# Reciprocal roots of the norms on GpSimd with a power instruction, in a two-layer decoder trunk on one core

## The chip, the core and the metric

The kernel runs on one core of a Trainium2 chip. The metric is the device time of one execution in microseconds (us), the median of a few runs. The core has a matrix engine (TensorE, PE in the profile, whose weight loads are PEld), three engines for other arithmetic (VectorE, DVE; ScalarE, ACT; GpSimd, POOL) and SyncE (SP), which issues most of the transfers. Each engine works through its own instructions in a fixed order; an instruction that needs another engine's result waits for a semaphore, and what stands behind it on its engine waits too.

## The reference

Two layers work on 256 tokens of width 1024. Each layer has four norms, before and after the mixer and before and after the MLP, and each is a mean of squares, a reciprocal root and a product:

```python
def _rms_norm(x, g):
    xf = x.astype(jnp.float32)
    y = xf * lax.rsqrt(jnp.mean(xf * xf, axis=-1, keepdims=True) + NORM_EPS)
    return (y * g.astype(jnp.float32)).astype(x.dtype)

def reference(x, w_in, ...):
    for l in range(DEPTH):
        h = _rms_norm(x, g_pre_mix[l])
        parts = jnp.split(h @ w_in[l], split_at, axis=-1)
        ...                                   # sparse attention and forgetting attention
        mix = jnp.concatenate([o_nsa, o_fox], axis=-1) @ w_out[l]
        x = x + _rms_norm(mix, g_post_mix[l])
        h = _rms_norm(x, g_pre_mlp[l])
        y = jnp.square(jax.nn.relu(h @ w_up[l])) @ w_down[l]
        x = x + _rms_norm(y, g_post_mlp[l])
    return x
```

## The kernel before

The 256 tokens are two tiles of 128 rows, t = 0 and 1; a row's square sum is one number per partition, so a reciprocal root is an instruction on a 128x1 operand. Weights come in by DMA as float32 (`wraw`) and are split into a rounded part `whi` (ScalarE) and a rest `wlo` (VectorE, `wlo<-wraw,whi`, two operands in SBUF); each float32 product is then made of fast matmuls on such parts. PSUM banks have four names: `acc`, `x`, `s` and `o`.

No engine's order is written by hand. The kernel's functions record every operation with a `Recorder`; a list scheduler with estimated costs (`_cost`) and due times (`deadlines`) orders all of them, and `RANKS`, a table of (operation number, rank), overrides the rank of single operations at the end. `emit` then writes the operations in that order, so every instruction has the line of `emit` and is told apart by the names of its tiles.

`rsqrt_sum(a, b, eps)` makes 1/sqrt(a + b + eps) from the two halves of a row's square sum. It is called twelve times:

- `first_factors` (layer 0): the squares of the input are summed over the features by a product with a column of one half (`s<-halves,squares`, four small products), copied to `half_sums` by VectorE, and give the factors of both tiles, `r_mix`. `row_scales` turns them into a row on PE (`s<-cst,rsqrt`), and ScalarE and VectorE scale the first chunk's products with them (`kv_tok`, `kS`, `vS`).
- `sandwich` (four times each layer: t = 0 and 1, after the mixer and after the MLP): ScalarE squares the two halves of the product, `acc[0]` and `acc[1]`, with a row sum into `sq` (written `rl,sq`); VectorE makes `mg = acc * gain`; `rsqrt_sum` makes r; VectorE makes `mg = mg * r + xo` in four pieces of 128x256, and PE transposes them (`s<-cst,mg`, four at a time) for the next stage's `xT`. Later X is updated by `x<-m,rsqrt,x`. At the end of the kernel (`store`) there is no next stage: X is updated and stored. There one half of tile 0 is scaled on ScalarE (`m<-m,rsqrt`) and added on GpSimd (`x<-x,m`).
- layer 1's first chunk: `r_mix` from the squares of X (`rms`).

GpSimd otherwise has sixteen AFFINE_SELECT instructions (the causal mask on the `bias` tiles) and 32 DMA issues, 16 a layer, that add a second read of a weight onto `wlo`.

Of the kernel before, what the change touches and what calls it, by code (L numbers as in the profile page):

```python
# [20 lines left out]
AF = mybir.ActivationFunctionType  # L21
OP = mybir.AluOpType
PSUM = bass.MemoryType.PSUM

P = 128
# [30 lines left out]
            "pr", "prT", "x0", "x1", "fV", "hs", "cs", "pcT", "vbig", "vS", "vW", "kstk", "kstv", "rT")  # L56
PAIRS = ("NSSSSSSSSSSSSN", "NSSSSSSSSSSSSSS")
RANKS = (
    (1199, 97914), (1855, 142093), (2445, 288237), (2467, 296098), (2485, 289771), (2685, 346998), (2881, 331053),
    (3625, 402769.65), (3673, 397125), (3771, 402770), (3934, 412549), (4853, 4861), (4862, 4865.000235571775),  # L60
    (4866, 4865), (4868, 574540),
)
EPS = 1e-6

# [133 lines left out]
class Recorder:  # L198
# [21 lines left out]
    def add(self, engine, name, args, kw):  # L220
# [14 lines left out]
        op.tile = _tile(op) if engine == "tensor" else None  # L235
        op.small = engine == "tensor" and not any(v.buf.name.startswith(("whi", "wlo")) for _, v in views)
        op.cost = _cost(op, views) + SLACK.get(engine, 0)
        deps = {} if self.after is None else {self.after: -1e9}
        op.bufs = []
# [245 lines left out]
def _product(name, args, side):  # L485

    n = int(np.prod(args[0].shape[1:]))
    rounded = args[1].dtype == F32R
    if name == "transpose":
        return 85.0 if rounded else 109.0  # L490
    if side > 1:
        return n / 2.4 + 20 if rounded else n / 0.6 + (60 if n >= 256 else 11)
    return max(118.0, n / 2.4 + (14 if n > 256 else 13)) if rounded else max(220.0, n / 0.6 + 7)


def _cost(op, views):

    out = op.args[0] if op.args else op.kw["out"]
    n = int(np.prod(out.shape[1:]))
    part = 100 * (out.shape[0] < P)  # L500
    if op.engine == "gpsimd":
        return 200 + 0.72 * n + 10 * int(np.prod(out.shape[1:-1]))
    if op.engine == "sync":
        v = views[0][1]
        return v.shape[0] * int(np.prod(v.shape[1:])) * 4 / 360.0
    if op.engine == "tensor":
        if op.name == "stretch":
            side = P // min(op.tile)
            return sum(_product(*x[:2], side) for x in op.args[2][::side])
        return _product(op.name, op.args, 1)  # L510
    if op.engine == "vector":
        if op.name == "reciprocal":
            return 60 + 6.5 * n
        if op.name == "tensor_reduce":
            n = int(np.prod(op.args[1].shape[1:]))
        fast = op.name in ("tensor_copy", "tensor_scalar", "memset") and not any(v.buf.psum for _, v in views)
        aps = sum(isinstance(v, View) for v in op.args[2:4]) if op.name == "tensor_scalar" else int(
            op.name == "scalar_tensor_tensor" and isinstance(op.args[2], View))
        return 68 + part + 64 * aps + n * (0.52 if fast else 1.04) + 10 * (op.name == "tensor_tensor_reduce")
    src = op.args[1]  # L520
    aps = sum(isinstance(op.kw.get(k), View) for k in ("bias", "scale", "accum_out"))
    return n / 1.2 + (55 if src.buf.psum else 92) + 93 * aps
# [94 lines left out]
def trunk(nc, A, consts_in, out, sbp, pp, dram):  # L617
    def tile(shape, dtype, name, tag=None, bufs=1):
        return nc.tile(sbp[(tag or name) not in OPERANDS], shape, dtype, name, tag, bufs)
# [4 lines left out]
    def small(shape, name, bufs=2):  # L624
        return tile(shape, F32, name=name, tag=name, bufs=bufs)
# [17 lines left out]
    for l in range(DEPTH):  # L643
# [28 lines left out]
        for u in range(len(PAIRS[l])):  # L672
            b = u % 2 * 2
# [6 lines left out]
        n = len(PAIRS[l])  # L680
# [9 lines left out]
    def weight(*key):  # L690
        return W.get(index[key])
# [13 lines left out]
    for k in range(8):  # L705
# [8 lines left out]
        a = 8 + k * NFIRST - o  # L714
# [18 lines left out]
        nc.tensor.matmul(ps[:, :n], warm[:, :P], warm[:, :n], start=True, stop=True)  # L733
    one_t = small([P, 1], "one", 1)
    nc.vector.memset(one_t, 1.0)
    kst = {}
    kbd = tile([P, 2, 2, 16], F32, name="kbd")
    vrep = tile([P, 2, 4, 2, 16], F32R, name="vrep")
# [29 lines left out]
        nc.scalar.activation(dst[0], src, AF.Copy)  # L768
        nc.vector.tensor_sub(dst[1], src, dst[0].bitcast(F32))

    def rsqrt_sum(a, b, eps=EPS, last=False):

        w = small([P, 5], "rsqrt", 6)
        c, d, y, t, r = (w[:, i:i + 1] for i in range(5))
        nc.vector.tensor_scalar(c, a, eps, None, op0=OP.add)
        nc.vector.tensor_scalar(d, c, -0.5, None, op0=OP.mult)
        nc.scalar.activation(y, b, AF.Ln, bias=c)
        nc.scalar.activation(y, y, AF.Exp, scale=-0.5)
        if last:
            nc.scalar.activation(t, b, AF.Identity, scale=-0.5, bias=d)  # L780
        else:
            nc.vector.tensor_scalar(t, b, -0.5, d, op0=OP.mult, op1=OP.add)
        nc.vector.scalar_tensor_tensor(t, y, t, y, op0=OP.mult, op1=OP.mult)
        nc.vector.scalar_tensor_tensor(r, t, 1.5, y, op0=OP.add, op1=OP.mult)
        return r

    def squares_of_x(t, tag):
# [13 lines left out]
    def to_xT(t, n, xg, xT):  # L801

        ps = psum("s")
        with nc.stretch():
            for k in range(4):
                nc.tensor.transpose(ps[:, k * P:k * P + P], xg[:, k * P:k * P + P], ident)
        split(ps.rearrange("p (k n) -> p k n", k=4), [y[:, 4 * n:4 * n + 4, t * P:t * P + P] for y in xT[:2]])
# [10 lines left out]
    def sandwich(t, acc, g_post, pre=None, xT=None, eps=EPS, store=None):  # L818


        sq = small([P, 2], "sq")
        m, mg = [None, None], [None, None]

        def times(name, n, gain):
            y = tokt(name)
            nc.vector.tensor_mul(y, acc[n], gain[:, half(n)])
            return y

        for n in range(2):
            junk = small([P, 512], "rl")  # L830
            nc.scalar.activation(junk, acc[n], AF.Square, scale=1.0 / 32.0, accum_out=sq[:, n:n + 1])
            if pre:
                mg[n] = times("mg", n, pre[0])
            if n == 0 and not pre:
                m[0] = times("m", 0, g_post)
        r = rsqrt_sum(sq[:, 0:1], sq[:, 1:2], eps, store is not None)
        if not pre:
            m[1] = times("m", 1, g_post)
        if pre:
            xg = []  # L840
            for n in range(2):
                xg.append(mg[n])
                for c in (0, 256):
                    a = n * 512 + c
                    nc.vector.scalar_tensor_tensor(xg[n][:, c:c + 256], mg[n][:, c:c + 256], r,
                                                   pre[1][t][:, a:a + 256], op0=OP.mult, op1=OP.add)
            yield
            for n in range(2):
                to_xT(t, n, xg[n], xT)
            yield  # L850
        for n in range(2):
            if pre:
                m[n] = times("m", n, g_post)
            if store is not None and t == 0 and n == 1:
                nc.scalar.activation(m[n], m[n], AF.Copy, scale=r)
                nc.gpsimd.tensor_add(X[t][:, half(n)], X[t][:, half(n)], m[n])
            else:
                nc.vector.scalar_tensor_tensor(X[t][:, half(n)], m[n], r, X[t][:, half(n)],
                                               op0=OP.mult, op1=OP.add)
            if store is not None:  # L860
                nc.sync.dma_start(store[:, half(n)], X[t][:, half(n)])
        yield
# [35 lines left out]
    def first_factors():  # L898
        ps = psum("s")
        for t in range(NT):  # L900
            nc.tensor.matmul(ps[:, t:t + 1], squares[:, t * P:t * P + P], half_t, start=True, stop=True)
        w = small([P, 2], "half_sums", 1)
        nc.vector.tensor_copy(w, ps[:, :2])
        return [rsqrt_sum(w[:, t:t + 1], w[:, t:t + 1]) for t in range(NT)]
# [5 lines left out]
    for l in range(DEPTH):  # L910
# [517 lines left out]
        if first:  # L1428
            for n, _ in enumerate(in_chunk(0, evac0)):
                if n == 11:  # L1430
                    nc.after = nc.ops[-1]
                    par.update(zip(("smT", "bias", "w2"), load_params(0)))
                    nc.sync.dma_start(cst[:, C_TRI:], consts_in[:, C_TRI:])
                    nc.after = None
                    r_mix = first_factors()
        else:

            for n, _ in enumerate(in_chunk(0, evac0, by_token=True)):
                if n == 6:
                    urgent(carry)  # L1440
                    next(carry)
                    for t in range(NT):
                        r_mix[t] = rsqrt_sum(*squares_of_x(t, "rm"))
# [257 lines left out]
        for u in range(len(PAIRS[l])):  # L1701
            fc, b = (u + 2) // 2, u % 2 * 2
# [7 lines left out]
            a = acts.pop(u)  # L1710
            w = W.pair(index[l, "dn", u // 2, b], PAIRS[l][u] == "S")
# [51 lines left out]
        n = len(PAIRS[l])  # L1763
        for u in range(n, 14):
# [3 lines left out]
            fc, b = u // 2, u % 2 * 2  # L1768
            act = [acts.pop(u)]
            for k in range(2):  # L1770
                w = weight(l, "dn", fc, b + k)
# [78 lines left out]
```

## Time and profile before

| | |
|---|---|
| median of 3 runs | 599.23 us (599.04 to 599.94) |
| span of the profiled execution | 597.2 us |
| PE busy | 589.6 us, 99% |
| DVE busy | 561.8 us, 94% |
| ACT busy | 493.0 us, 83% |
| POOL busy | 38.8 us, 6% |
| chain that ended last | 98% PE |
| mean granted TensorE clock | 0.998 |

The profile is of one execution; the span is from its first to its last instruction, and the 2.0 us to the median of the runs lie outside it (the page gives no other time of that execution). Busy time is a union of the instructions' spans. A matmul's end is modelled: 128x512 matmuls are listed with some 0.39 us but start 0.23 us apart, so PE that is shown as busy may still wait a little between two starts. The chain is followed back from the last instruction to what released each step.

### The profile page before, as it was taken

Reading aid. Unit: us, or ns where it says so; the run is one execution under the profiler, and the core shown is the slowest. Engines: PE = TensorE matmul, PEld = TensorE weight load, DVE = VectorE, ACT = ScalarE, POOL = GpSimd, SP = SyncE. Lnnn points to the kernel's source line nnn. Section 1 sums busy time; section 2 is a strip of 40 time slices with the busy share of each in tenths; the row PEclk is TensorE's granted clock in tenths of the full one; section 3 lists DMA queues with packets and bytes.
Section 4 is the critical chain, followed back from the end, with each engine's and each line's share of the span. In section 5 each row is a group of like instructions: output and inputs, shape, how many; then the busy total and the mean of one; then the engine's idle time right before and its main releaser. Section 6 shows DMA issues by size and latency. Waiting matters only on the chain.

```text
span 597.2 us, 9917 instructions
## 1 busy us (share of the span) xinstructions
PE 589.6 (99%) x3312; PEld 492.7 (82%) x3312; DVE 561.8 (94%) x1212; ACT 493.0 (83%) x899; POOL 38.8 (6%) x53
## 2 busy tenths in 40 slices
PE   9999999999999999999999999999999999999995
PEld 7988887788888888888888888777888888888884
DVE  7899999989999999999799999988999999999997
ACT  7677888677999999998667959884889999999984
POOL 0000200001100001010000021000110010101000
PEclk9999999999999999999999999999999999999999
DMA  8996629729988878989348762584598879887621
GB/s 318 380 356 196 262 83 299 259 70 294 282 238 284 237 252 255 277 246 289 112 138 280 256 207 109 165 295 142 130 299 248 276 231 287 235 271 239 181 36 71
DMA packets 39427, 135.64 MB, mean 227 GB/s; under 512 B 4656, under 2 KB 4816, under 8 KB 39376
## 3 DMA queue, kind: packets, MB, share of 16 engines
q1 hardware_dynamic: 34768, 118.23, 56.4%
q0 software_dynamic: 4608, 16.78, 15.7%
q8 instruction: 26, 0.43, 0.3%
q14 instruction: 25, 0.20, 0.1%
HBM read 133.92 MB, written 1.07 MB: 226 GB/s over the span
## 4 chain that ended last, share of the span: by engine, by line
PE 98%; DMA 1%; DVE 0%; ACT 0%; issue 0%; DVEq 0%
PE s L454 42%; PE acc L454 26%; PE x L454 21%; PE o L454 10%; DMA first<-in_first_dram 1%; DVE x L454 0%; DVE m L454 0%; DVEq L1846 0%; ACT xT L454 0%; DVE rsqrt L454 0%; ACT rl L454 0%
## 5 line engine op out<-in xcount | busy, mean ns | idle before, releaser
L454 ACT ACTIVATE whi<-wraw 128x1024 fp32r<-128x1024 f32 (+2 forms) x188 | 180.5, 978 | 18.4 <-PE acc L454 6.7
L454 DVE TENSOR_TENSOR wlo<-wraw,whi 128x1024 fp32r<-128x1024 f32 (+2 forms) x156 | 171.0, 1105 | 4.0 <-ACT whi L454 3.5
L454 PE MATMUL s<-xT,whi 128*128 128x512 f32 x448 | 111.2, 390 | 0.0
L454 PEld LDWEIGHTS s<-xT,whi 128*128 128x128 f32 x448 | 83.9, 188 | 17.6
L454 DVE TENSOR_TENSOR wlo<-wsum,whi 128x1024 fp32r<-128x1024 f32 x52 | 63.4, 1221 | 2.4 <-ACT whi L454 2.1
L454 PEld LDWEIGHTS s<-xT,wlo 128*128 128x128 f32 x448 | 61.1, 190 | 4.4
L454 PE MATMUL s<-xT,wlo 128*128 128x256 f32 x448 | 62.5, 282 | 0.0
L454 ACT ACTIVATE whi<-wsum 128x1024 fp32r<-128x1024 f32 x52 | 55.0, 1057 | 8.9 <-PE s L454 8.6
L454 POOL DMA_DIRECT2D wlo<-in_w_up_dram x32 | 27.9, 872 | 384.7 <-ACT wlo L454 159.7
L454 PE MATMUL x<-whi,aS 128*128 128x512 f32 x128 | 49.2, 391 | 0.0
L454 ACT ACTIVATE pr<-pr,st 128x256 f32<-128x256 f32 (+1 forms) x96 | 42.8, 449 | 6.8 <-DVE st L454 6.8
L454 PE MATMUL acc<-whi,aS 128*128 128x512 f32 x128 | 45.9, 392 | 0.0
L454 PE MATMUL s<-whi,aS 128*128 128x512 f32 x104 | 37.6, 391 | 0.0
L454 DVE TENSOR_TENSOR wsum<-wraw,wsum 128x512 f32<-128x512 f32 x52 | 35.8, 688 | 0.8
L454 PE MATMUL x<-whi,xT 128*128 128x512 f32 x112 | 35.6, 395 | 0.4 <-ACT xT L454 0.4
L454 PE MATMUL acc<-whi,xT 128*128 128x512 f32 (+1 forms) x128 | 35.6, 350 | 0.0
L454 ACT ACTIVATE y<-s 128x512 f32<-128x512 f32 x56 | 32.7, 584 | 2.8 <-PE s L454 2.4
L454 ACT ACTIVATE wlo<-wraw 128x1024 fp32r<-128x1024 f32 x32 | 33.6, 1051 | 1.4 <-PE o L454 1.1
L454 PE MATMUL acc<-xT,whi 128*128 128x512 f32 x128 | 34.3, 397 | 0.0
L454 DVE TENSOR_TENSOR wsum<-wraw 128x1024 f32<-128x1024 f32 x26 | 31.7, 1220 | 0.0
L454 DVE TENSOR_TENSOR aS<-quads,aS 128x896 fp32r<-128x896 f32 (+3 forms) x31 | 31.4, 1013 | 0.0
L454 ACT ACTIVATE aS<-quads 128x896 fp32r<-128x896 f32 (+3 forms) x31 | 27.5, 887 | 4.2 <-DVE quads L454 3.7
(259 smaller groups left out, 1271.7 us busy)
## 6 DMA issues: line engine op xcount, KB each, us to landing
wraw<-in_w_up_dram SPq DMA_DIRECT2D x64, 512.0 KB, 5.3
wraw<-in_w_down_dram SPq DMA_DIRECT2D x64, 512.0 KB, 5.9
wraw<-in_w_in_dram SPq DMA_DIRECT2D x36, 512.0 KB, 5.2
wlo<-in_w_up_dram POOLq DMA_DIRECT2D x32, 512.0 KB, 7.0
wraw<-in_w_out_dram SPq DMA_DIRECT2D x16, 512.0 KB, 4.1
w<-in_cmp_w_k_dram SPq DMA_DIRECT2D x8, 512.0 KB, 6.0
w<-in_cmp_w_v_dram SPq DMA_DIRECT2D x8, 512.0 KB, 5.8
bias<-sums SPq DMA_DIRECT2D x8, 384.0 KB, 5.3
```

What stands on the lines that cost most here:

```text
L454: getattr(getattr(self.nc, op.engine), name)(*[real(v) for v in args], **{k: real(v) for k, v in kw.items()})
```

## The change

`rsqrt_sum` had two VectorE instructions that prepare (`a + eps` and its product with -0.5), a logarithm and an exponential on ScalarE, and a Newton step of three VectorE instructions (in the last norm one of them on ScalarE). Now it has three GpSimd instructions: `c = a + eps`, `d = b + c`, `r = d ^ -0.5`, the last a TENSOR_TENSOR whose second operand is a 128x1 tile `power` that VectorE fills once. The cost rule of the scheduler gets another estimate for TENSOR_TENSOR on GpSimd. `RANKS` holds other entries, 42 where there were 15, and with this the whole order is another.

```diff
+    (10, 8.9985), (15, 43116.8677), (17, 43116.8654), (20, 1529.1849), (56, 54.0011), (61, 64.0017),
...
     if op.engine == "gpsimd":
+        if op.name == "tensor_tensor" or op.name == "tensor_add":
+            return 200 + 2.1 * n
         return 200 + 0.72 * n + 10 * int(np.prod(out.shape[1:-1]))
...
+    power = small([P, 1], "power", 1)
+    nc.vector.memset(power, -0.5)
...
-    def rsqrt_sum(a, b, eps=EPS, last=False):
-        w = small([P, 5], "rsqrt", 6)
-        c, d, y, t, r = (w[:, i:i + 1] for i in range(5))
-        nc.vector.tensor_scalar(c, a, eps, None, op0=OP.add)
-        nc.vector.tensor_scalar(d, c, -0.5, None, op0=OP.mult)
-        nc.scalar.activation(y, b, AF.Ln, bias=c)
-        nc.scalar.activation(y, y, AF.Exp, scale=-0.5)
-        if last:
-            nc.scalar.activation(t, b, AF.Identity, scale=-0.5, bias=d)
-        else:
-            nc.vector.tensor_scalar(t, b, -0.5, d, op0=OP.mult, op1=OP.add)
-        nc.vector.scalar_tensor_tensor(t, y, t, y, op0=OP.mult, op1=OP.mult)
-        nc.vector.scalar_tensor_tensor(r, t, 1.5, y, op0=OP.add, op1=OP.mult)
+    def rsqrt_sum(a, b, eps=EPS):
+        w = small([P, 3], "rsqrt", 6)
+        c, d, r = (w[:, i:i + 1] for i in range(3))
+        nc.gpsimd.tensor_scalar(c, a, eps, None, op0=OP.add)
+        nc.gpsimd.tensor_scalar(d, b, c, None, op0=OP.add)
+        nc.gpsimd.tensor_tensor(r, d, power, op=OP.pow)
         return r
...
-        r = rsqrt_sum(sq[:, 0:1], sq[:, 1:2], eps, store is not None)
+        r = rsqrt_sum(sq[:, 0:1], sq[:, 1:2], eps)
```

In the rows of the orders below, a name before the arrow is written and the names behind it are read; xN stands for N alike in a row.

The first place is `first_factors`. On VectorE, around the copy of the sums (`half_sums`), before:

```order
L454 COPY half_sums<-s 128x2
L454 TENSOR_TENSOR wlo<-wraw,whi 128x576
L454 TENSOR_SCALAR rsqrt<-half_sums 128x1 x2
L454 TENSOR_SCALAR rsqrt<-rsqrt 128x1 x2
L454 TENSOR_SCALAR rsqrt<-half_sums,rsqrt 128x1 x2
L454 TENSOR_TENSOR wlo<-wraw,whi 128x1024
L454 SCALAR_TENSOR_TENSOR rsqrt<-rsqrt 128x1 x4
L454 TENSOR_SCALAR vS<-x,rsqrt 128x128 x2
```

Now, on the same engine:

```order
L459 TENSOR_TENSOR wlo<-wraw,whi 128x576
L459 COPY half_sums<-s 128x2
L459 TENSOR_TENSOR wlo<-wraw,whi 128x1024
L459 TENSOR_SCALAR vS<-x,rsqrt 128x128 x2
L459 TENSOR_TENSOR rope<-kS,cst 128x32
```

The ten small instructions of the two roots are gone from VectorE, and a 128x1024 split stands right behind the copy. GpSimd has these at its start, ahead of its masks:

```order
L459 TENSOR_SCALAR rsqrt<-half_sums 128x1 x2
L459 TENSOR_SCALAR rsqrt<-half_sums,rsqrt 128x1 x2
L459 TENSOR_TENSOR rsqrt<-rsqrt,power 128x1 x2
L459 AFFINE_SELECT bias<-bias 128x2x128 x8
```

On PE, what now stands between the products that sum the squares (`s<-halves,squares`, right ahead of the first row here) and the turn of the roots into a row (`s<-cst,rsqrt`):

```order
L459 MATMUL acc<-whi,xT 128x288
L459 MATMUL acc<-wlo,xT 128x288
L459 MATMUL acc<-whi,xT 128x288 x2
L459 MATMUL acc<-wlo,xT 128x288
L459 MATMUL acc<-whi,xT 128x288 x2
L459 MATMUL acc<-wlo,xT 128x288
L459 MATMUL acc<-whi,xT 128x288 x2
L459 MATMUL acc<-wlo,xT 128x288
L459 MATMUL acc<-whi,xT 128x288 x2
L459 MATMUL acc<-wlo,xT 128x288
L459 MATMUL acc<-whi,xT 128x288
L459 MATMUL s<-cst,rsqrt 128x128 x2
```

That is 15 matmuls; before, 30 such matmuls stood there.

The second place is `sandwich` after the mixer of layer 0, tile 0 (banks `x`). On VectorE before:

```order
L454 TENSOR_TENSOR mg<-x,gains 128x512
L454 TENSOR_SCALAR rsqrt<-sq 128x1
L454 TENSOR_SCALAR rsqrt<-rsqrt 128x1
L454 TENSOR_TENSOR mg<-x,gains 128x512
L454 TENSOR_SCALAR rsqrt<-sq,rsqrt 128x1
L454 SCALAR_TENSOR_TENSOR rsqrt<-rsqrt 128x1 x2
L454 SCALAR_TENSOR_TENSOR mg<-mg,rsqrt,xo 128x256 x3
```

Now:

```order
L459 TENSOR_TENSOR mg<-x,gains 128x512
L459 TENSOR_TENSOR wsum<-wraw 128x1024
L459 TENSOR_TENSOR mg<-x,gains 128x512
L459 SCALAR_TENSOR_TENSOR mg<-mg,rsqrt,xo 128x256 x4
L459 TENSOR_TENSOR wlo<-wraw,whi 128x1024
```

The small instructions are gone, and a 128x1024 sum of weights stands between the two `mg`. On PE the first transposition `s<-cst,mg` of this place stood behind 16 matmuls into `acc` that follow the last one into `x`; now it stands behind 13.

The third place is the end of the kernel. ScalarE before:

```order
L454 ACTIVATE rl,sq<-x 128x512 x2
L454 ACTIVATE rsqrt<-sq,rsqrt 128x1 x2
L454 ACTIVATE rsqrt<-rsqrt 128x1
L454 ACTIVATE rl,sq<-acc 128x512
L454 ACTIVATE m<-m,rsqrt 128x512
L454 ACTIVATE rl,sq<-acc 128x512
L454 ACTIVATE rsqrt<-sq,rsqrt 128x1 x2
L454 ACTIVATE rsqrt<-rsqrt 128x1
```

ScalarE now, where the product with r comes ahead of both squares of tile 1:

```order
L459 ACTIVATE aT<-h_6911 128x512
L459 ACTIVATE wsum<-x 128x512
L459 ACTIVATE rl,sq<-x 128x512 x2
L459 ACTIVATE m<-m,rsqrt 128x512
L459 ACTIVATE rl,sq<-acc 128x512 x2
```

On GpSimd the addition `x<-x,m` was the last instruction; now it stands between the roots of the two tiles:

```order
L459 TENSOR_SCALAR rsqrt<-sq,epsr 128x1
L459 TENSOR_SCALAR rsqrt<-sq,rsqrt 128x1
L459 TENSOR_TENSOR rsqrt<-rsqrt,power 128x1
L459 TENSOR_TENSOR x_808<-x_808,m 128x512
L459 TENSOR_SCALAR rsqrt<-sq,epsr 128x1
L459 TENSOR_SCALAR rsqrt<-sq,rsqrt 128x1
L459 TENSOR_TENSOR rsqrt<-rsqrt,power 128x1
```

The root of tile 1 thus waits on GpSimd for the addition of tile 0.

More of the change, by code (lines that the diff above doesn't have):

```diff
@@ L58 @@
 RANKS = (
-    (1199, 97914), (1855, 142093), (2445, 288237), (2467, 296098), (2485, 289771), (2685, 346998), (2881, 331053),
-    (3625, 402769.65), (3673, 397125), (3771, 402770), (3934, 412549), (4853, 4861), (4862, 4865.000235571775),
-    (4866, 4865), (4868, 574540),
[8 rows of a table added]
 )
```

7 rows, old and new, of the table RANKS are left out of this document.

## The prediction

> **What bounds the kernel now.** I read the busy shares first, then the chain of waits by engine, then PE's own waits, then the span in three windows (before PE's first real product, to the end of its last, and the rest).
>
> ```profile
> span 597.2 us, 9917 instructions
> PE 589.6 (99%) x3312; PEld 492.7 (82%) x3312; DVE 561.8 (94%) x1212; ACT 493.0 (83%) x899; POOL 38.8 (6%) x53
> PE 98%; DMA 1%; DVE 0%; ACT 0%; issue 0%; DVEq 0%
> PE o L454 <- PEq L1840: 0.8, 1, 0.8
> PE x L454 <- ACT xT L454: 0.4, 1, 0.4
> ...
> 4.87:590.74 585.87, 585.87 (x3302) 489.74 (x3302) 557.75 (x1200) 489.91 (x892) 37.34 (x48) 1.00 0.73 228
> 590.74:597.20 6.46, 0.00 (x1) 0.00 (x0) 3.03 (x7) 1.26 (x5) 1.27 (x1) 0.78 0.44 164
> ```
>
> The chain lies on PE for 98%. PE waited 1.2 us in all (us in total, times, longest), of which 0.8 us before the program's first product; that leaves 0.4 us between 4.87 and 590.74. In the window rows the first number is the length and the second PE's busy time: PE fills 585.87 us of 585.87, at a granted clock of 1.00. The two orders hold the same 3312 matmuls in the same shapes. So the change can't shorten the middle by more than that one wait of 0.4 us and some 0.1 us of changes from one bank to another; everything else that it can do there is to make PE wait for a root. A gain must come from the 6.46 us after PE, where the last root stands.
>
> **What is removed.** Per root two small VectorE instructions and a Newton step go, and a logarithm and an exponential on ScalarE (in the rows on one tile: fewest, median and most ns):
>
> ```profile
> L454 DVE SCALAR_TENSOR_TENSOR rsqrt<-rsqrt x24: 145/185/220, 20.2 to 592.4; 128x1 f32<-128x1 f32 x24
> L454 DVE TENSOR_SCALAR rsqrt<-sq,epsr x4: 204/206/208, 293.7 to 590.5; 128x1 f32<-128x1 f32 x4
> L454 ACT ACTIVATE rsqrt<-rsqrt x12: 186/203/205, 19.0 to 591.9; 128x1 f32<-128x1 f32 x12
> ```
>
> About five VectorE instructions of 0.15 to 0.2 us and two of ScalarE, twelve times: some 10 us of VectorE and 6 us of ScalarE work. Of that nothing counts in itself, since PE hides both engines outside the end of the kernel: I put it at 0.
>
> **What is added: the price on GpSimd.** The trace of before has no 128x1 arithmetic and no power on POOL. The nearest rows:
>
> ```profile
> L1840 POOL MEMSET const-float32-0.0<- 128x1 f32 x1 | 0.1, 99 | 0.2 <-issue 0.2
> L454 POOL TENSOR_SCALAR_AFFINE_SELECT bias<-bias x16: 404/432/1537, 58.9 to 361.6; 128x256 f32<-128x256 f32 x16
> L454 POOL TENSOR_TENSOR x<-x,m 128x512 f32<-128x512 f32 x1 | 1.3, 1269 | 19.4 <-ACT m L454 19.4
> 58.68 1.21 DVE L454 TENSOR_TENSOR wlo<-wraw,whi 128x1024 fp32r<-128x1024 f32 x1
> 58.91 1.25 POOL L454 TENSOR_SCALAR_AFFINE_SELECT bias<-bias 128x256 f32<-128x256 f32 x1 [58.46 <-DVE st L454]
> 65.56 0.42 DVE L454 TENSOR_TENSOR fkT<-acc,fkT 128x256 f32<-128x256 f32 x1
> 65.56 0.41 POOL L454 TENSOR_SCALAR_AFFINE_SELECT bias<-bias 128x256 f32<-128x256 f32 x1 [5.05 <-PE acc L454]
> 354.82 1.54 POOL L454 TENSOR_SCALAR_AFFINE_SELECT bias<-bias 128x256 f32<-128x256 f32 x1 [3.67 <-ACT cs L454]
> 354.86 1.22 DVE L454 TENSOR_TENSOR wlo<-wraw,whi 128x1024 fp32r<-128x1024 f32 x1
> ```
>
> From below: a MEMSET of 128x1 takes 0.10 us. From above: an AFFINE_SELECT of 256 columns takes 0.41. One column with an operand to read lies nearer to the MEMSET; I take 0.2 us for each of the three, the power included, and keep 0.10 and 0.41 for the range. A product on ScalarE that ended at 590.72 let GpSimd start at 590.80 (rows of the end, below), so a hop between engines is 0.08.
>
> The same fence shows a second cost. The AFFINE_SELECT of 0.41 us took 1.25 and 1.54 us where VectorE ran `wlo<-wraw,whi`, with both operands in SBUF, and ended 0.27 us behind it (58.91 + 1.25 = 60.16 against 59.89; 356.36 against 356.08). Beside a VectorE product that reads one operand from PSUM (`fkT<-acc,fkT`) it took 0.41. So GpSimd stood still until VectorE's instruction had ended.
>
> **The first factors (layer 0).** Before:
>
> ```profile
> 17.18 0.50 PE L454 MATMUL s<-halves,squares 128*128 128x1 f32 x4
> 17.72 0.16 DVE L454 COPY half_sums<-s 128x2 f32<-128x2 f32 x1
> 17.80 0.76 DVE L454 TENSOR_TENSOR wlo<-wraw,whi 128x576 fp32r<-128x576 f32 x1
> ...
> 21.61 0.38 PE L454 MATMUL s<-cst,rsqrt 128*128 128x128 f32 x2
> ```
>
> PE starts the sums at 17.18 and turns the roots at 21.61, 4.43 us later, with 30 matmuls of 288 columns between: less 0.4 for the four small products, 0.134 each. Now 15 stand between, so the first turn is due 4.43 - 15 x 0.134 = 2.42 us after the sums, the second 0.1 later. What the roots need: the copy starts 0.54 after the sums; the 128x1024 split that now follows on VectorE starts 0.08 behind it, as `wlo` does at 17.80, and takes 1.22, to 1.84. The first c is released at about 0.78, into the split, and is held to its end; half its own 0.2 remains (1.94). Five more instructions make 1.0, and the hop 0.1: 3.04, against 2.52. That makes PE wait 0.5 us. At 0.10 per instruction it is 0, at 0.41 it is 1.7 (1.84 + 0.28 + 2.05 + 0.1 - 2.52).
>
> The rule for this is in the Trainium skill, page "SBUF — State Buffer", section "Who interferes with whom": a VectorE instruction with two inputs in SBUF contends with a GpSimd instruction that reads SBUF, and whoever issues first holds the shared ports to its end. The trace agrees (1.25 us against 0.41). By the rule the sum has the 0.5 above and the time is 599.5; without it the roots would be there at 0.78 + 1.2 + 0.1 = 2.1, the wait would be 0 and the time 599.0.
>
> **The roots in the middle.** Layer 0 after the mixer, tile 0, is the tightest kind:
>
> ```profile
> 122.00 0.62 PE L454 MATMUL acc<-whi,oT 128*128 128x512 f32 x2
> 122.20 0.60 ACT L454 ACTIVATE rl<-x 128x512 f32<-128x512 f32 x1 [0.22 <-PE x L454]
> 122.70 0.20 ACT L454 ACTIVATION_READ_ACCUMULATOR rl<-x 128x1 f32 x1
> 124.29 1.28 DVE L454 SCALAR_TENSOR_TENSOR mg<-mg,rsqrt,xo 128x256 f32<-128x256 f32 x3
> 125.64 0.60 PE L454 MATMUL s<-cst,mg 128*128 128x128 f32 x4
> ```
>
> From the first matmul behind the bank's end (122.00) to the first transposition were 3.64 us and 16 matmuls; with 13 it is 3.64 - 3 x 0.228 = 2.96 (3.64 over 16 is 0.228 each). Counted from the bank's end, the square sum is out at 0.90. GpSimd's c would start at 0.98, but VectorE's new `wsum<-wraw` of 128x1024 stands between the two `mg`, and it too reads SBUF twice. By the order the first half's bank ends seven matmuls sooner (-1.6); its square sum (0.2 + 0.8) is out at -0.6, `mg` takes 0.69 and the sum, with the 1.21 of `wlo`, runs from 0.1 to 1.3. So c is held to 1.3 and ends at 1.4, r at 1.8, with a hop 1.9. The second `mg` runs from 1.3 to 2.0, so the root is no later than that; two pieces of three in 1.28 are 0.86 and a hop makes 2.94, against 2.96: no wait, and nothing to spare. At 0.41 r comes at 2.5: a wait of 0.5. The two other places of tile 0 have 13 matmuls too and no such sum: 0.98 + 0.6 + 0.08 = 1.66, with 0.94 for pieces and hop 2.6; at 0.41 3.23, a wait of 0.27 each. Tile 1 has 3.0 to 3.5 us, some 0.3 in all at 0.41. So 0 at 0.2 us, and 1.3 at 0.41. PE's matmuls hide these roots; without them the pieces and transpositions would be late by what is missing. On GpSimd itself a root would be late behind its DMA issues, but they lie elsewhere:
>
> ```profile
> 70.17 0.77 POOL L454 TENSOR_SCALAR_AFFINE_SELECT bias<-bias 128x256 f32<-128x256 f32 x2 [1.13 <-DVE gz L454]
> 130.88 1.01 POOL L454 DMA_DIRECT2D wlo<-in_w_up_dram  x1 [59.95 <-DVE mg L454]
> 273.51 0.88 POOL L454 DMA_DIRECT2D wlo<-in_w_up_dram  x1 [6.71 <-ACT wlo L454]
> 349.91 1.24 POOL L454 TENSOR_SCALAR_AFFINE_SELECT bias<-bias 128x256 f32<-128x256 f32 x2 [75.52 <-DVE gh L454]
> ```
>
> Layer 0's last mask is at 70, its first DMA issue comes behind the roots after the mixer (122 to 130), the last ends some 20 us before the roots of the MLP (293.7, among the removed rows above).
>
> **The end of the kernel.**
>
> ```profile
> 588.56 0.20 ACT L454 ACTIVATION_READ_ACCUMULATOR rl<-x 128x1 f32 x1
> 590.01 0.71 ACT L454 ACTIVATE m<-m,rsqrt 128x512 f32<-128x512 f32 x1
> 590.78 0.60 ACT L454 ACTIVATE rl<-acc 128x512 f32<-128x512 f32 x1
> 590.80 1.27 POOL L454 TENSOR_TENSOR x<-x,m 128x512 f32<-128x512 f32 x1 [19.44 <-ACT m L454]
> 591.27 0.19 ACT L454 ACTIVATION_READ_ACCUMULATOR rl<-acc 128x1 f32 x1
> 591.50 0.69 DVE L454 TENSOR_TENSOR m<-acc,gains 128x512 f32<-128x512 f32 x1
> 592.55 1.42 DVE L454 SCALAR_TENSOR_TENSOR x<-m,rsqrt,x 128x512 f32<-128x512 f32 x2
> ```
>
> Before, the last square sum was out at 591.46 and its root let VectorE start at 592.55: 1.09 us. Three instructions and two hops would be 0.76. But two other things come in. ScalarE now does `m<-m,rsqrt` ahead of both squares of tile 1: tile 0's sum is out at 588.76, its root at 588.76 + 0.76 = 589.52, `m` at 590.23, and two squares of 0.68 each (590.78 to 591.46) end at 591.60. And GpSimd adds `x<-x,m` ahead of the three instructions: 590.31 to 591.58, just in time. So the root is there at 591.60 + 0.76 = 592.36, and the last product starts 0.2 us sooner. At 0.10 it is 0.33 sooner, where `m<-acc,gains` (to 592.19) becomes the later of the two. At 0.41 (1.39 with hops) the same working gives root 590.15, `m` 590.86, squares 592.22, root 593.6: 1.1 later.
>
> **The sum.** 0.5 - 0.2 = +0.3 on a span of 597.2. The median of the runs lies 2.03 above that span, and the page gives no other time of this execution, so I carry the difference over: 597.5 + 2.0 = 599.5. All at 0.10, with PE's wait of 0.4 and the bank changes of 0.1 gone too: 0 - 0.33 - 0.5 = -0.8, 598.4. All at 0.41: 1.7 + 1.3 + 1.1 = +4.1, 603.3.
>
> **Rivals.** Slow power (slower): one instruction, `r = d ^ -0.5`, is not like an addition but takes as long on one column as POOL's addition on 512 takes, 1.27 us, 1.07 more than assumed. At the first factors it stands twice in the chain (0.5 + 2.1 = 2.6), at the end its two roots add up (2.0 with the working above), and six sandwiches miss 0.2 to 0.7 each (3.4): +8.0, 607. For it speaks that no row shows a power on POOL; against it that the long row has 512 columns. It decides from 0.42 us for the power alone: at 0.22 too much, four times in the two tight places (0.88), with +0.3, it passes 1.2 us. All three alike pass it from 0.28. A dearer first call belongs here: the first AFFINE_SELECT took 0.84 more than a free one, which VectorE's split explains, since that at 354.82 wasn't the first and took longer; 0.84 more at the first factors would be 600.3. The Trainium skill ("GPSIMD Engine Reference", "Instruction dispatch") gives some 6 us for the first call of freshly loaded code; no row here shows one, and the sum with it would be 605.
>
> No block, or cheap instructions: the copy's release comes first, or 0.10 us is the price. Then PE doesn't wait: 598.4 to 599.0, still no measurable change. For it speak the MEMSETs; against it the two blocked AFFINE_SELECT.
>
> Faster by over 0.2%, which is 1.2 us and about what a measurement of this kernel can tell from no change: it needs the whole 0.33 at the end, the 0.4 of PE's wait, and 0.5 more from waits that the profile doesn't list, some gap in PE's starts: 598.0 or less. Against it stands 585.87 of 585.87.
>
> **How the numbers follow.** My case, a wait of half a microsecond at the first factors nearly paid back at the end: 0.40, 599.5. No block or cheap: 0.22. Instructions of 0.28 to 0.41 us, +1.2 to +4: 0.20. Slow power or a first call of microseconds: 0.10. Faster than 598.0: 0.08. So faster 0.08, within 0.2% 0.62, slower 0.30. The range 598.4 to 603.3 takes the ends of the unknown price and leaves out the slow power and most of the faster case.
>
> **What would show it.** Right: from the start of `s<-halves,squares` to `s<-cst,rsqrt` about 2.9 us, with PE waiting some 0.5 for the root; the first GpSimd instruction on `half_sums` over 0.8 us long and the other five about 0.2; no new PE waits at `s<-cst,mg`; last `x<-m,rsqrt,x` within 0.9 us of the last square sum. Wrong: a power of 0.4 us or more, PE waits at many `s<-cst,mg`, or an addition `x<-x,m` that holds the last root.

## The result, and the profile after

The changed kernel takes 606.46 us (median of four runs, 606.25 to 607.04) against 599.59 us for the kernel before on the same chip: ratio 1.0118, 95% interval 1.0105 to 1.0130, so 6.9 us slower. I had predicted 599.5 us, with a range up to 603.3 and a chance of 0.30 for slower. The profiled execution has a span of 604.8 us against 597.2, 7.6 us more.

The page of the changed kernel begins, and PE's waits are:

```profile
span 604.8 us, 9887 instructions
PE 592.9 (98%) x3312; PEld 494.9 (82%) x3312; DVE 553.8 (92%) x1155; ACT 487.7 (81%) x873; POOL 56.8 (9%) x89
PE 95%; POOL 2%; DVE 1%; ACT 1%; issue 0%; POOLq 0%; DVEq 0%; ACTq 0%
PE s L459 <- POOL rsqrt L459: 3.8, 4, 2.6
PE o L459 <- PEq L1842: 0.8, 1, 0.8
```

VectorE has 8.0 us less to do (561.8 to 553.8) and ScalarE 5.3 less, and nothing came of it. POOL, which had no share in the chain that ends last, now has 2%. PE's list of waits names the cause: four waits for a root that GpSimd makes, 3.8 us in all, one of them 2.6. All four are at `s<-cst,rsqrt`, two at the first factors of layer 0 and two at layer 1's first chunk; no transposition `s<-cst,mg` of the six sandwiches in the middle is among them.

The costs of GpSimd's instructions, on one tile (fewest, median and most ns, first and last start):

```profile
L459 POOL TENSOR_TENSOR rsqrt<-rsqrt,power x12: 550/567/572, 21.9 to 599.6; 128x1 f32<-128x1 f32 x12
L459 POOL TENSOR_SCALAR rsqrt<-sq,rsqrt x8: 282/282/397, 125.8 to 599.2; 128x1 f32<-128x1 f32 x8
L459 POOL TENSOR_SCALAR rsqrt<-sq x4: 221/222/676, 124.1 to 428.9; 128x1 f32<-128x1 f32 x4
```

The first instruction takes 0.22 us, the second 0.28, the power 0.57: 1.07 for the three, where I had 0.6. And one second instruction, at layer 1's first chunk, takes 4.46 us. The timeline there (start, length, instruction):

```profile
309.54 1.41 DVE L459 SCALAR_TENSOR_TENSOR x<-m,rsqrt,x 128x512 f32<-128x512 f32 x2
310.45 4.46 POOL L459 TENSOR_SCALAR rsqrt<-rms,rsqrt 128x1 f32<-128x1 f32 x1 [1.34 <-ACT rl L459]
310.86 3.90 DVE L459 TENSOR_TENSOR wlo<-wraw,whi 128x576 fp32r<-128x576 f32 x5
312.64 0.39 PE L459 MATMUL x<-whi,xT 128*128 128x512 f32 x1
315.61 0.32 PE L459 MATMUL s<-cst,rsqrt 128*128 128x128 f32 x1 [2.59 <-POOL rsqrt L459]
316.95 0.32 PE L459 MATMUL s<-cst,rsqrt 128*128 128x128 f32 x1 [0.22 <-POOL rsqrt L459]
```

GpSimd's instruction starts at 310.45, while VectorE is in the second of seven instructions that follow each other without a break (309.54 to 314.76) and all read two operands from SBUF. It ends at 314.91, behind the last of them. The power follows, and PE turns the root at 315.61, 3 us after the start of its last other matmul (312.64). What came behind that wait stands in the windows (length, PE, PEld, DVE, ACT and POOL busy, granted clock, DMA):

```profile
312.00:315.60 3.60, 1.02 (x5) 0.52 (x3) 2.76 (x4) 0.64 (x4) 3.47 (x2) 1.00 0.82 265
315.60:317.20 1.60, 1.36 (x9) 1.13 (x10) 0.16 (x1) 1.60 (x3) 1.07 (x3) 1.00 0.86 241
317.20:320.60 3.40, 3.40 (x17) 3.39 (x16) 2.78 (x7) 2.88 (x6) 0.00 (x0) 0.51 1.02 377
```

For 3.4 us PE ran at a granted clock of 0.51: about 3.4 x 0.49 = 1.7 us more lost, without any wait.

The first factors and the end of the kernel, which answer to the rows shown of before:

```profile
19.06 0.50 PE L459 MATMUL s<-halves,squares 128*128 128x1 f32 x4
19.60 0.16 DVE L459 COPY half_sums<-s 128x2 f32<-128x2 f32 x1 [1.31 <-PE s L459]
19.68 1.23 DVE L459 TENSOR_TENSOR wlo<-wraw,whi 128x1024 fp32r<-128x1024 f32 x1
19.85 1.14 POOL L459 TENSOR_SCALAR rsqrt<-half_sums 128x1 f32<-128x1 f32 x1 [19.42 <-DVE half_sums L459]
21.38 0.54 POOL L459 TENSOR_SCALAR rsqrt<-half_sums,rsqrt 128x1 f32<-128x1 f32 x2
21.87 1.09 POOL L459 TENSOR_TENSOR rsqrt<-rsqrt,power 128x1 f32<-128x1 f32 x2
22.50 0.32 PE L459 MATMUL s<-cst,rsqrt 128*128 128x128 f32 x1 [0.84 <-POOL rsqrt L459]
23.02 0.32 PE L459 MATMUL s<-cst,rsqrt 128*128 128x128 f32 x1 [0.20 <-POOL rsqrt L459]
...
597.27 0.39 PE L459 MATMUL acc<-whi,aT 128*128 128x512 f32 x1
597.57 1.26 POOL L459 TENSOR_TENSOR x<-x,m 128x512 f32<-128x512 f32 x1 [0.84 <-ACT m L459]
598.44 0.20 ACT L459 ACTIVATION_READ_ACCUMULATOR rl<-acc 128x1 f32 x1
598.81 0.29 POOL L459 TENSOR_SCALAR rsqrt<-sq,epsr 128x1 f32<-128x1 f32 x1
...
600.16 1.42 DVE L459 SCALAR_TENSOR_TENSOR x<-m,rsqrt,x 128x512 f32<-128x512 f32 x2 [0.78 <-POOL rsqrt L459]
```

At the first factors the split that follows the copy holds the first instruction from 19.85 to 20.99 (0.22 without it), and the first turn comes 3.44 us after the sums; 2.42 were free. The second turn is 0.52 behind the first instead of 0.1. That is 1.4 us. At the end the last square sum is out at 598.64 and the product starts at 600.16, 1.52 us later; it was 1.09. From the start of PE's last matmul to the end of the span it is 604.8 - 597.27 = 7.5 us, against 597.2 - 590.36 = 6.8: 0.7 more.

So the 7.6 us are: first factors 1.4; layer 1's first chunk 3.0 of lateness at the two turns and 1.7 of slow clock, 4.7 in all; the end 0.7. The rest, 0.8, is mostly of two parts. PE's first matmuls ran slowly for 0.4 us longer than in the profile of before (the second pair started at 5.85 instead of 5.50); profiles of the kernels below show between 0 and 0.5 of it, so it isn't the change. Some 0.3 lies near 50 us; it is there in every kernel below that has the new order and makes the first factors' roots on GpSimd, and gone where VectorE and ScalarE make them, and I haven't followed it further.

### The profile page after: what moved, and what is told of

Read it like the earlier page. It is cut to its first block, busy times and chain, and to the rows that moved or that the text cites. A ratio compares the mean times of both kernels' runs of the same rounds, so it can differ in the third digit from the quotient of the medians.

```text
span 604.8 us, 9887 instructions
## 1 busy us (share of the span) xinstructions
PE 592.9 (98%) x3312; PEld 494.9 (82%) x3312; DVE 553.8 (92%) x1155; ACT 487.7 (81%) x873; POOL 56.8 (9%) x89
## 3 DMA queue, kind: packets, MB, share of 16 engines
HBM read 133.92 MB, written 1.07 MB: 223 GB/s over the span
## 4 chain that ended last, share of the span: by engine, by line
PE 95%; POOL 2%; DVE 1%; ACT 1%; issue 0%; POOLq 0%; DVEq 0%; ACTq 0%
PE s L459 41%; PE acc L459 24%; PE x L459 19%; PE o L459 11%; POOL rsqrt L459 2%; DVE wlo L459 0%; DVE qS L459 0%; ACT rl L459 0%; POOL x L459 0%; ACT whi L459 0%; DVE fqT L459 0%; DVE x L459 0%; ACT m L459 0%; DVEq L1848 0%; POOLq L1848 0%
```

## The experiments

The theory: GpSimd's instructions read SBUF, and while VectorE works through instructions with two operands in SBUF, one behind the other, they stand still; at the two places where PE has little other work this decides, and a wait of over 2 us also lowers PE's clock. Two rivals: the power's own price makes the loss; the new order of the whole program does, whoever makes the roots.

**The new order with the old roots.** All twelve chains back on VectorE and ScalarE, in the changed kernel's order:

```diff
-        nc.gpsimd.tensor_scalar(c, a, eps, None, op0=OP.add)
-        nc.gpsimd.tensor_scalar(d, b, c, None, op0=OP.add)
-        nc.gpsimd.tensor_tensor(r, d, power, op=OP.pow)
+        # in their places: c, d | Ln, Exp, t | the two steps of Newton
```

> The changed kernel's order, but all twelve roots made as before by VectorE and ScalarE (logarithm, exponential, Newton step), put where the GpSimd instructions stood; the two of the first factors right behind the copy of the sums. Theory (GpSimd's instructions are held by trains of VectorE instructions with two SBUF operands, and are dearer than assumed): the loss goes with GpSimd, so 599 to 600.5 us, PE waits for roots at most 1 us in all, no slow clock at 316 to 321 us. Rival 1 (the new order itself costs, whoever makes the root): 604 to 606. Rival 2 (the power's own 0.57 us is the loss): the same 599 to 600.5, it is told apart by the next kernels.

It took 604.13 us (ratio 1.0074, 1.0059 to 1.0089). My theory's figure is missed, and the time lies in the range of the rival that the new order costs (604 to 606). PE no longer waits at the first factors and there is no slow clock, but the old chains, dropped into places laid out for three instructions, are late elsewhere:

```profile
PE s L494 <- DVE rsqrt L494: 1.3, 1, 1.3
PE s L494 <- DVE mg L494: 0.6, 2, 0.3
```

The 1.3 us are at layer 1's first chunk, where ScalarE's logarithm stood behind a weight split of 1.06 us, and the end was 1.3 us longer than before. The kernel doesn't tell theory and order apart, since it tests my placement as well; the next ones do.

**A multiplication for the power.** The root is left out; every instruction, place and wait stays.

```diff
-        nc.gpsimd.tensor_tensor(r, d, power, op=OP.pow)
+        nc.gpsimd.tensor_tensor(r, d, power, op=OP.mult)
```

> The changed kernel with a multiplication in place of the power (this leaves out the root, so the numbers it makes are another's; every instruction, wait and place is the same). The TENSOR_TENSOR on 128x1 takes about 0.3 us in place of 0.57. Theory (blocked instructions): the waits for blocked instructions stay, so only 0.3 to 0.5 us less at each of the first factors, layer 1's first chunk and the end: 605.2 to 605.9 us, the second instruction of layer 1's first root still over 4 us long. Rival (the power's price makes the loss): 600 to 602.

603.16 us (ratio 1.0054, 1.0033 to 1.0074): 3.3 us less than the changed kernel. Neither figure was met.

```profile
L472 POOL TENSOR_TENSOR rsqrt<-rsqrt,power x12: 191/192/194, 21.5 to 597.1; 128x1 f32<-128x1 f32 x12
309.29 4.44 POOL L472 TENSOR_SCALAR rsqrt<-rms,rsqrt 128x1 f32<-128x1 f32 x1 [1.38 <-ACT rl L472]
PE s L472 <- POOL rsqrt L472: 2.6, 2, 2.2
```

The power costs 0.57 - 0.19 = 0.38 us more than a product on one column. By the times of PE's starts it is in series twice at the first factors (0.75 gained there) and twice at the end (0.7 gained), and shortens the wait and the slow clock at layer 1 (0.8 together). About 0.4 more is the start of PE's clock in that profile. So the power's price is a real part, some 2.3 us. But the blocked instruction is as long as it was, 4.44 us, and PE still waits 2.2 us for it.

**Breaks in VectorE's train.** MEMSETs between the five splits at layer 1's first chunk:

```diff
+        for op, n in zip(wlo[k:], (1, 3, 2, 2)):      # the first four of the five splits
+            for _ in range(n):
+                ops.insert(ops.index(op) + 1, self.made("vector", "memset", self.gap, 0.0))
```

> The changed kernel with eight MEMSETs of 128x192 put on VectorE between the five weight splits at layer 1's first chunk (1, 3, 2 and 2 of them behind the first four). They are extra work, about 1.6 us, but a MEMSET reads no SBUF. Theory (GpSimd gets no turn between two VectorE instructions that follow each other with two SBUF operands): the instruction of 4.46 us ends in the first gap, at about 312 us instead of 314.9, the power in the second, and PE waits for this root under 0.8 us instead of 2.6; with no long wait no slow clock follows: 602 to 603.5 us. Rival (something else delays that instruction, or GpSimd is served between two instructions anyway): nothing won, 606 to 607.

602.93 us (ratio 1.0056, 1.0041 to 1.0071): eight instructions more on VectorE, and 3.5 us faster than the changed kernel.

```profile
309.96 2.05 POOL L477 TENSOR_SCALAR rsqrt<-rms,rsqrt 128x1 f32<-128x1 f32 x1 [1.34 <-ACT rl L477]
310.39 0.74 DVE L477 TENSOR_TENSOR wlo<-wraw,whi 128x576 fp32r<-128x576 f32 x1
311.12 0.22 DVE L477 MEMSET gap<- 128x192 f32 x1
311.26 0.69 DVE L477 TENSOR_TENSOR wlo<-wraw,whi 128x576 fp32r<-128x576 f32 x1
311.94 0.87 DVE L477 MEMSET gap<- 128x192 f32 x3
312.10 0.57 POOL L477 TENSOR_TENSOR rsqrt<-rsqrt,power 128x1 f32<-128x1 f32 x1
312.72 0.32 PE L477 MATMUL s<-cst,rsqrt 128*128 128x128 f32 x1 [0.18 <-POOL rsqrt L477]
```

The instruction ends at 312.01 instead of 314.91, and PE's wait for this root is 0.18 us. The second tile's root still waits 1.2 us, behind the later splits, so the gain is at the lower end. The granted clock behind it stays at 1.00. This shows that the train holds this instruction back: nothing else was taken away. I had the gap wrong: the single MEMSET, 0.13 us between two splits, wasn't enough, and the instruction ended 0.07 us into the gap of three.

The same with MEMSETs of 128x1:

```diff
-                ops.insert(ops.index(op) + 1, self.made("vector", "memset", self.gap, 0.0))
+                ops.insert(ops.index(op) + 1, self.made("vector", "memset", self.gap[:, :1], 0.0))
```

> As the kernel with eight MEMSETs between the splits of layer 1's first chunk, but each of 128x1 in place of 128x192, so that they take about 0.06 us each. If GpSimd needs only a break in the train: the second instruction ends in the first gap, at about 312 us as there, and the time is 602 to 603 us, no longer than with the long MEMSETs. If it needs a gap as long as its own reading (0.2 us or more) it gets no turn: the instruction takes over 4 us, 605.5 to 607.

603.31 us (ratio 1.0074, 1.0051 to 1.0098), 0.3 above my figure. A break is enough for the first tile: the instruction took 1.91 us and ended behind the second split, at three MEMSETs that together leave 0.2 us; the single MEMSET ahead of them left nothing, as the second split starts (311.01) before the first ends (311.09). But the second tile's power took 1.56 us: it started 0.09 us into the last two splits, which follow each other at once, and ended at 315.40, behind the first of them (314.97) and well ahead of the end of the second (316.11). PE waited 1.8 us for it, and that wait left the granted clock at 1.00 in this profile.

And with products of one operand in SBUF in place of the MEMSETs:

```diff
-                ops.insert(ops.index(op) + 1, self.made("vector", "memset", self.gap, 0.0))
+                ops.insert(ops.index(op) + 1, self.made("vector", "tensor_scalar", self.gap, self.gap, 2.0, None, op0=OP.mult))
```

> As the kernel with eight MEMSETs of 128x192 between the splits of layer 1's first chunk, but with products of a 128x192 tile in SBUF by a constant in their place (one operand read from SBUF, result in SBUF). If only instructions with two SBUF operands hold GpSimd off: as there, the instruction of 4.46 us takes about 2 us, 602.5 to 603.5 us. If a product with one SBUF operand holds it off too: over 4 us, with a train 1.3 us longer, 606.5 to 608.

602.64 us (ratio 1.0052, 1.0037 to 1.0067), no different from the MEMSETs within the intervals. (One MEMSET more, ahead of the train at 308.73, fills the tile that the products read.)

```profile
310.13 1.42 POOL L478 TENSOR_SCALAR rsqrt<-rms,rsqrt 128x1 f32<-128x1 f32 x1 [1.31 <-ACT rl L478]
311.39 0.27 DVE L478 TENSOR_SCALAR gap<-gap 128x192 f32<-128x192 f32 x1
```

The instruction ended at 311.55, during the first of these products. The power behind it met the next split, which ended at 312.32, and was done 0.50 us later, beside the three products: they cost it nothing. So it isn't VectorE's being busy that holds GpSimd's instruction, nor its reading SBUF. Nor is it the length of VectorE's instructions alone: at the end of the changed kernel the first of the three (598.81) took its usual 0.29 us beside a `m<-acc,gains` of 0.68 us, which has one operand in PSUM. What remains, and what all that held it share, is two operands from SBUF.

**The split at the first factors moved behind what waits for the roots.**

```diff
+        ops.remove(wlo)                               # the split behind the copy of the sums
+        ops.insert(ops.index(vS) + 1, wlo)            # behind the second vS
```

> The changed kernel with the 128x1024 split that stands right behind the copy of the sums on VectorE (first factors) moved behind the two vS, which wait for the roots. Theory: the first GpSimd instruction there takes 0.21 us instead of 1.14, the roots come 0.9 us sooner, PE's waits of 0.84 and 0.20 there fall to 0.3 or less: 605.2 to 605.8 us, if the split isn't late in its turn. Rival (the prices of the six instructions make the wait): the waits shrink by under 0.3 us, 606.2 or more.

606.07 us (ratio 1.0105, 1.0090 to 1.0120), within the noise of the changed kernel and between the two figures. The block went as expected: the first two instructions took 0.52 us together instead of 1.43 and PE's waits there fell from 1.04 to 0.2. But the split was then late:

```profile
19.63 0.52 POOL L477 TENSOR_SCALAR rsqrt<-half_sums 128x1 f32<-128x1 f32 x2 [19.20 <-DVE half_sums L477]
PE s L477 <- POOL rsqrt L477: 2.8, 2, 2.6
PE s L477 <- DVE qS L477: 0.4, 1, 0.4
PE s L477 <- DVE pcs L477: 0.3, 1, 0.3
```

0.7 us of new waits for VectorE's later work took back nearly all of the 0.8 won. That is what my edit cost, not a sign against the block; the time alone would have misled.

**Old roots at layer 1's first chunk only; there and at the first factors; and the same with ScalarE's part earlier.** The other eight or ten roots stay on GpSimd.

```diff
+            if n not in (6, 7):            # of the twelve roots; next: (0, 1, 6, 7)
+                continue
```

> The changed kernel with only the two roots of layer 1's first chunk made as before, on VectorE and ScalarE; the other ten stay on GpSimd. Theory (the held instruction there and the slow clock behind it cost 4.6 us): 601.7 to 602.6 us, granted clock 1.00 between 308 and 320 us, PE waits there under 0.5 us. Rival (the loss is spread over the roots, by the price of their instructions): at most 2 us won, 604.5 or more.

603.27 us (ratio 1.0069, 1.0044 to 1.0094), 3.2 us less than the changed kernel. The slow clock is gone, the held instruction too, but the old chain is itself 1.3 us late here (the logarithm behind the weight split again), and this profile has a wait of 0.9 us for VectorE's `pcs` that the two next kernels don't have. The figure was missed by 0.7 us; these two would account for it, but the four runs themselves lie between 602.35 and 605.40.

> The changed kernel with the four roots of the first factors and of layer 1's first chunk made as before; the eight of the sandwiches stay on GpSimd. Theory: what is left over the kernel before is the end (0.7 us) and some 0.3 us of the order: 600.2 to 601.2 us; the six GpSimd roots in the middle cost PE nothing (no wait for mg over 0.1 us). Rival (the middle roots or the new order cost too): 602 or more.

601.05 us (ratio 1.0028, 1.0018 to 1.0038). PE's whole list of waits:

```profile
PE s L496 <- DVE rsqrt L496: 1.3, 1, 1.3
PE o L496 <- PEq L1880: 0.8, 1, 0.8
```

The figure was met. Eight roots are on GpSimd, in the new order, and PE doesn't wait for one of them.

```diff
+                at = max(at, ops.index(pre[1])) + 1   # behind ScalarE's square of the second half
+                ops[at:at] = mid[:2]                  # logarithm and exponential
```

> As the kernel with the four roots of the first factors and of layer 1's first chunk made as before, but with ScalarE's logarithm and exponential of the latter ahead of the weight split that held them by 1.06 us. Theory (all that the change loses in the middle lies at these two places): PE's wait of 1.3 us for the root falls to 0.7 or less, nothing else moves, 599.8 to 600.6 us; what is left over the kernel before is the end with its 0.7 us. Rival (something else in the new order costs): 601 us or more.

600.41 us (ratio 1.0022, 1.0012 to 1.0032), as expected, with a wait for that root of 0.7 us. What is left over the kernel before is that and the end, whose 7.5 us behind PE's last matmul start are those of the changed kernel. This closes the account: in the middle the new order costs nothing that these runs resolve, and the change loses at two places and at the end.

**The old order with GpSimd's roots.** The kernel before, with three instructions in the places of seven and nothing else:

```diff
+            ops[ops.index(seven[0])] = mk("gpsimd", "tensor_scalar", c, a, eps, None, op0=OP.add)
+            ops[i:i + 1] = [mk("gpsimd", "tensor_scalar", d, b, c, None, op0=OP.add),
+                            mk("gpsimd", "tensor_tensor", r, d, self.power, op=OP.pow)]
```

> The kernel before, in its own order, with GpSimd's three instructions in the places of the seven, and nothing else changed. Theory: at the first factors, where 30 matmuls stand, nothing is lost; at layer 1's first chunk the second instruction meets a train of two x<-m,rsqrt,x and three splits, each with two SBUF operands, so it takes over 2.5 us and PE waits 1.5 us or more for the root, with a slow clock behind; the end loses 0.5 to 1: 602 to 605 us. Rival (the new table of ranks is what costs): 599.5 to 600.3.

603.26 us (ratio 1.0062, 1.0041 to 1.0084).

```profile
18.00 0.76 DVE L479 TENSOR_TENSOR wlo<-wraw,whi 128x576 fp32r<-128x576 f32 x1
18.17 0.67 POOL L479 TENSOR_SCALAR rsqrt<-half_sums 128x1 f32<-128x1 f32 x1 [17.74 <-DVE half_sums L479]
18.68 1.22 DVE L479 TENSOR_TENSOR wlo<-wraw,whi 128x1024 fp32r<-128x1024 f32 x1
312.03 4.96 POOL L479 TENSOR_SCALAR rsqrt<-rms,rsqrt 128x1 f32<-128x1 f32 x1 [0.43 <-ACT rl L479]
312.76 4.16 DVE L479 TENSOR_TENSOR wlo<-wraw,whi 128x576 fp32r<-128x576 f32 x4
PE s L479 <- POOL rsqrt L479: 1.6, 1, 1.6
PE s L479 <- DMA wlo<-in_w_up_dram: 0.5, 1, 0.5
```

The order theory falls: the ranks are the old ones and the loss is 3.7 us. The first factors are blocked here too, but 30 matmuls hide it. The rows also set a limit to the theory: the first instruction on `half_sums` ended at 18.85, 0.09 us behind the first split, although the second split had followed at once (18.68 to 19.89). Only the next GpSimd instruction, which started into the second split, waited for its end. Layer 1's first chunk meets another train (4.96 us), PE waits 1.6 us, and the clock stays at 1.00 behind it, where I had expected a slow one. The wait of 0.5 us for a weight's second read I had not expected, and its cause I didn't look for.

The order does have a share: with the old one the roots on GpSimd cost 3.7 us, with the new one 6.9, and the profiles put nearly all of the difference at two places: 1.4 at the first factors, where it leaves 15 matmuls instead of 30, and 1.7 of slow clock at layer 1.

## Why the prediction was wrong

- **Removed work at 0: right.** VectorE and ScalarE gave up 13 us, and PE's stream took nothing from it.
- **The price on GpSimd: mis-sized.** I took 0.2 us for each of the three. The first was 0.22, the second 0.28, the power 0.57. I put "the power included" at the price of an addition, and the multiplication that took its place at 0.19 us shows that for it alone this was wrong. The rival of a slow power named 0.42 us as its point, and 0.57 is beyond it.
- **The first factors: mechanism right, size off.** The block came as worked out (0.08 us past the end of the split, 20.99 against 20.91). I forecast a wait of 0.5; the turns are 1.0 and 1.4 us late. The difference is the price of the five instructions behind it.
- **The middle roots at 0: right.** Layer 0's tile 0 after the mixer is as tight as worked out, though by another path:

```profile
124.70 0.62 PE L459 MATMUL acc<-whi,oT 128*128 128x512 f32 x2
126.72 1.67 DVE L459 SCALAR_TENSOR_TENSOR mg<-mg,rsqrt,xo 128x256 f32<-128x256 f32 x4 [0.26 <-POOL rsqrt L459]
127.65 0.60 PE L459 MATMUL s<-cst,mg 128*128 128x128 f32 x4
```

From 124.70 to 127.65 are 2.95 us, where I had 2.96; VectorE waited 0.26 us for the root and PE not at all. I had the first instruction held by the sum between the two `mg`; it ran before that sum began (124.09 to 124.31), and the second one waited for ScalarE's square sum until 125.75. That the dearer power still fitted is luck: an instruction that was done early paid for it.
- **Layer 1's first chunk: the step that failed.** The prediction goes through the first factors, the six sandwiches in the middle and the end; the two roots of layer 1's first chunk stand in no term of it, and so were put at 0 without a reason, also at the dear end. What I used at the first factors, GpSimd stands still beside two SBUF operands, was not tried on the train of seven such instructions there. The runs show 3.0 us of lateness in its place: the second instruction took 4.46 us, and 1.42 to 2.05 once the train had breaks.
- **The slow clock: missing from the prediction.** No wait in the kernel before is long enough to show it. It cost 1.7 us.
- **The end: wrong sign.** I forecast 0.2 us less; it is 0.7 more. The order of events was as worked out (ScalarE's product, GpSimd's addition, then the three instructions); at 1.07 us for the three the last root comes 1.5 us after its square sum instead of 0.76. In part a sign of being wrong that I had named came true: the addition ran to 598.83, so the first of the three, which needs only the sum of the first half (out at 598.06), started behind it, 0.17 us after the last sum. The last sum itself also came 0.3 us later behind PE's last matmul than before.
- **The rivals.** The time is nearly that of the slow power (607), but not by its sum: that had 3.4 us at the sandwiches, where PE lost nothing, and nothing at layer 1's first chunk, where it lost most. A figure that comes out right by another sum isn't a hit.

The Trainium skill ("SBUF — State Buffer", "Who interferes with whom") says that a VectorE instruction with at most one SBUF input, outside the modes that use both of VectorE's ports, doesn't contend with GpSimd. The products with one operand let the instruction through (1.42 us against 4.46), so the runs agree; whether those products ran in such a mode no run here shows.

## What to carry to other kernels

A small instruction on GpSimd is only as quick as VectorE's order lets it be: before moving a root or a scale there, list what VectorE does at every place where it is due, and look for runs of instructions with two operands in SBUF. Only one form of instruction, the one with a column as operand, was held through whole trains; whether another form in its place would have come through no run here tests. Test a rule found at one place at all the others, first where the busiest engine has little other work. And give an operation that the trace doesn't show a price of its own: the power was 0.38 us dearer than the product, in series four times where it mattered.

## What the runs showed of the hardware

- A 128x1 TENSOR_SCALAR on GpSimd with a column as second operand got no turn between VectorE instructions with two operands in SBUF that follow each other at once: it took 4.46 and 4.96 us behind trains, 0.28 where nothing held it. A gap of some 0.2 us let it through. Of the shorter gaps, two MEMSETs of 128x1 (0.14 us) and one product with a single SBUF operand (0.11 us from the end of one split to the start of the next) did, and one MEMSET (0.13 us) didn't. Why these differ is open.
- Other forms did get a turn between two such instructions: the addition of a constant in the old order (0.09 us behind the end of the first of two splits), the power in the kernel with MEMSETs of 128x1 (0.43 us behind), and in the kernel before a mask (361.00 to 361.68), 0.27 us behind the first of two `pcs<-cs,pcs`, while the second ran to 361.95. What makes the difference no run here tests.
- A power on 128x1 takes 0.57 us on GpSimd, a product 0.19, an addition of a constant 0.22, with a column as operand 0.28.
- After PE had waited 2.6 us (changed kernel, and the one with the split moved; 2.2 in the kernel with the product), the granted clock fell to a half; in the changed kernel this was 1.6 us after work resumed, for 3.4 us. After waits of 1.2, 1.6 and 1.8 us it stayed at 1.00. The Trainium skill ("TensorE: Matmul & The Clock Gate", "Part 1: The HAM clock gate") gives an idle window of about 3.4 us for the fall to half clock. The half and the 3.4 us agree; here less than a whole window of idling was enough.
- The length of the wait isn't all that counts: in each profile the clock changed only at whole steps of 3.413 us counted from its first rise (changed kernel: rise at 6.65, falls at 317.26 and 600.56, 91 and 174 steps later). In the middle of the program it fell behind steps in which PE stood idle for 2.0, 2.2 and 2.5 us (changed kernel, product, split moved), and not behind one with 1.6 (MEMSETs of 128x1), the most without a fall; the wait of 1.6 us in the old order lay across two steps, with 0.7 and 0.9 us. So the place of a wait in the steps counts too, and it seems to differ from run to run: two of the four runs with the product have a mean granted clock of 0.994 and take 603.8 us, the other two 0.996 and 0.999 and at most 602.6.
